# Blocks of the conditioning matrices on ScalarE's transfer queue

## The chip, the cores and the metric

One core of a Trainium2 chip runs the whole kernel in one launch. The metric is device time in microseconds (us), the median of several runs. Five engines matter: TensorE (PE) multiplies, VectorE (DVE) and ScalarE (ACT) do elementwise work, GpSimd (POOL) does sums over partitions and a few powers, and SyncE (SP) only issues transfers. ACT can issue transfers too. Each engine takes its instructions in the order in which they stand in its own stream.

## The reference

An input x of 512 tokens with 1024 features goes through two blocks, each modulated by a conditioning vector c.

```
first block, mod = silu(c) @ ada_w + ada_b        (1024 x 9*1024, cut into 9 pieces sh, sc, g)
  y = rmsnorm(h, g_pre) * (1 + sc1) + sh1
  h = h + 0.5 * g1 * rmsnorm(swiglu(y, w_gate, w_up, w_down), g_post)
  y = rmsnorm(h) * (1 + sc2) + sh2;   h = h + g2 * rmsnorm(mlstm_and_hgrn(y @ w_in) @ w_out)
  a second swiglu with sh3, sc3, g3
second block, twice: mod = silu(c) @ ada_w[l] + ada_b[l]     (1024 x 6*1024, 6 pieces)
  h = h + g * mixer(rmsnorm(h) * (1 + sc) + sh)    (l = 0: gated linear attention,
                                                     l = 1: differential attention)
  h = h + g * (relu(y @ mlp_w1) ** 2) @ mlp_w2     (hidden width 4096)
a final rmsnorm
```

All matrices are float32.

## The kernel before, in words

Every large product is made of three products of a coarse and a fine half of both operands: `fm` (L372 to L374) with the weights as the stationary operand, `tm` (L390 to L392) with the activations as that. A weight matrix comes in `raw` tiles of 1 MB (L333 in `group`, L348 in `group_k`; two buffers). ACT copies the coarse half into a `w` tile (L118 is the line of every ACT instruction), DVE subtracts it from the raw tile for the fine half (L328). There are six `w` tiles. The activations of a layer are kept transposed, in pairs of coarse and fine tiles (`XA...`, `XB...`); L471 and L472 make such a pair from ACT's result `RS`, L611 and L612 (or L606 and L612) make the hidden ones from `tmp`.

The conditioning vectors are made on the side, since each is one row times a matrix of 1024 x 1024. `ada_steps` makes eight steps of each, two halves of 512 columns by four blocks of 256 rows. A step transfers its block of 512 KB into an `araw` tile (L237, two buffers, which the bias rows of L257 and L259 share) and has DVE multiply and add its two halves of 128 rows into `acc` (L241 for the first of a half, L245 for the others). After the fourth block of a half POOL sums `acc` over the partitions (L253), and DVE picks out or adds the bias (L260 to L268). 152 blocks are transferred so. The steps are queued in `jobs`; `work`, called with every product with an estimate of its length, takes one off each 8 us (feed-forward) or 16 us (mixers), so the blocks are spread over the program. The first two pieces of the first block's modulation are needed at once and are made from other strips (L676, eight of them, added by L681 and L683 and summed on PE at L686), which stand with the input and the first weights at the head of SP's stream.

A scheduler sets the order of every engine's stream from the program and from its own estimate of durations; a changed queue therefore moves other instructions too. PSUM has eight banks. In the feed-forward layers six of them hold results of products until ACT or DVE has read them; in the differential attention fewer do: `DIFF_IN_BANKS` names four and `DIFF_BANKS` two. There `d_proj` makes values, queries and keys for four heads at a time; `rope` has ACT copy a product to `tmp` and DVE turn it (L1448 to L1451), PE transposes it (L1546) and ACT copies it into `Y` or `XB`. `diff_X` transposes finished heads (L1525, L1528).

Of the kernel before, what the change touches and what calls it, by code (L numbers as in the profile page):

```python
# [35 lines left out]
def kernel(ctx: ExitStack, tc: tile.TileContext, a: dict, out: bass.AP):  # L36
    nc = tc.nc
# [30 lines left out]
    def sl(tag, dt=F32, w=512):  # L68
        if tag in fixed:
            t = fixed[tag][dt == F32R]  # L70
            return (t if dt in (F32, F32R) else t.bitcast(dt))[:, 0:w]
        return tp.tile([128, w], dt, tag=tag, name=tag, bufs=1)

    def tl(dt=F32, w=512):
        return tp.tile([128, w], dt, tag="tmp", name="tmp", bufs=NTMP)

    def sm(w, tag="sm", bufs=NSM):
        return tp.tile([128, w], F32, tag=tag, name=tag, bufs=bufs)

    def ct(shape, name, dt=F32):  # L80
        return const.tile(shape, dt, tag=name, name=name)
# [23 lines left out]
    def after(ins, first):  # L105
        tc.add_manual_dep(ins.ins, first.ins.name,
                          mybir.DependencyInfo(mybir.DependencyClass.NoSync, mybir.DependencyReason.DATA),
                          reason="activation table")
# [117 lines left out]
    def ada_steps(w, c0, sc, bias, name, post=None, f=1.0):  # L226


        st = {}

        def step(half, kk):
            if kk == 0:
                st["acc"] = tp.tile([128, 512], F32, tag="acc", name="acc", bufs=1)
            acc = st["acc"]
            c = c0 + half * 512
            raw = rawp.tile([128, 2, 512], F32, tag="araw", name="araw", bufs=2)
            nc.sync.dma_start(raw, w[kk * 256:(kk + 1) * 256, c:c + 512].rearrange("(k p) f -> p k f", p=128))  # L237
            for k in range(2):
                col = sc[:, kk * 2 + k:kk * 2 + k + 1]
                if kk == 0 and k == 0:  # L240
                    i = V.tensor_scalar(acc, raw[:, 0, :], col, None, op0=ALU.mult)  # L241
                    if gate:
                        after(i, gate.pop())
                else:
                    V.scalar_tensor_tensor(acc, raw[:, k, :], col, acc, op0=ALU.mult, op1=ALU.add)  # L245
            if kk < 3:
                return
            row = len(bias.shape) == 1
            if half == 0:
                st["r"] = sl("rb", w=D) if row else ct([128, KD], name)  # L250
            r = st["r"]
            red = tl()
            G.partition_all_reduce(red, acc, channels=128, reduce_op=bass_isa.ReduceOp.add)  # L253
            if row:
                hs = slice(half * 512, half * 512 + 512)
                rt = rawp.tile([128, 2, 512], F32, tag="araw", name="araw", bufs=2)
                nc.sync.dma_start(rt[:, 0, :], bias[hs].partition_broadcast(128))  # L257
                if post is not None:
                    nc.sync.dma_start(rt[:, 1, :], post[hs].partition_broadcast(128))  # L259
                V.tensor_tensor(r[:, hs], red, rt[:, 0, :], op=ALU.add)  # L260
                if post is not None:
                    V.scalar_tensor_tensor(r[:, hs], r[:, hs], f, rt[:, 1, :], op0=ALU.mult, op1=ALU.mult)
            else:
                rv = red.rearrange("p (m q) -> p m q", q=128)
                V.tensor_tensor(rv, rv, ident.unsqueeze(1).to_broadcast([128, 4, 128]), op=ALU.mult)
                c4_ = sm(8)[:, 0:4]
                V.tensor_reduce(c4_, rv, axis=AX.X, op=ALU.add)
                V.tensor_tensor(r[:, half * 4:half * 4 + 4], c4_, bias[:, half * 4:half * 4 + 4], op=ALU.add)  # L268
            if half == 1:
                mods[name] = r  # L270
        return [lambda a=a, b=b: step(a, b) for a in range(2) for b in range(4)]

    def bg(n=1):
# [1394 lines left out]
```

## Time and profile before

| | |
|---|---|
| median of 3 runs | 2285.28 us (2283.25 to 2286.25) |
| the profiled execution | 2286.35 us, its span 2284.6 us |
| PE busy | 2225.5 us (97%) |
| DVE busy | 1416.6 us (62%) |
| ACT busy | 923.5 us (40%) |
| POOL busy | 190.2 us (8%) |
| moved by the transfers | 294.69 MB, mean 129 GB/s |
| transfers of the page's list at L237 | 152 of 512 KB, on SP |

The profile is that of one execution. Its times start with the span. A row of the timeline gives the start, the duration, the engine, the line, the operation and the tiles it writes and reads; in square brackets stands how long the engine had been idle before and what it waited for. SPq and ACTq are the issues of transfers: their duration is the issue, not the transfer. When a transfer has landed is seen where an engine that waited for it starts.

### The profile page before, as it was taken

To read this page: it belongs to the slowest core of one execution; us is meant where nothing else is said; L and a number is where in the kernel's file an instruction comes from. 1 tells how busy PE (TensorE), PEld (TensorE's weight loads), DVE (VectorE), ACT (ScalarE), POOL (GpSimd) and SP (SyncE) were. 2 spreads that over 40 slices of the span, in tenths; PEclk is the share of its full clock that TensorE was granted. 3 is DMA by queue.
4 is the path that set the end of the run, shared out by engine and by line. 5 is a ranking of instruction groups with operands and counts; after the bars stand their busy time and mean duration, and the time that the engine had idled before them with its cause. 6 is when DMAs were issued, how large, how long until landed. Compare 5 with 4: busy or idle time off the path is not lost.

```text
span 2284.6 us, 27962 instructions
## 1 busy us (share of the span) xinstructions
PE 2225.5 (97%) x10904; PEld 1839.5 (81%) x10904; DVE 1416.6 (62%) x2371; ACT 923.5 (40%) x1722; POOL 190.2 (8%) x126
## 2 busy tenths in 40 slices
PE   6999999999899999999999999999999999999998
PEld 4888888888788888888888887888776767988887
DVE  7856465765777746555554775568756577634465
ACT  4332234644665332234544443222445456433223
POOL 0111111000101111010000011011000000100000
PEclk9999999999999999999999999999999999999999
DMA  9755454446223655452332254445431311523231
GB/s 272 242 181 181 149 166 74 111 106 105 95 75 111 206 167 179 130 166 76 127 122 92 88 175 156 148 153 157 132 125 55 115 65 50 163 93 102 92 96 61
DMA packets 212900, 294.69 MB, mean 129 GB/s; under 512 B 7257, under 2 KB 120328, under 8 KB 212768
## 3 DMA queue, kind: packets, MB, share of 16 engines
q1 hardware_dynamic: 212128, 291.85, 42.1%
q8 instruction: 85, 1.39, 0.3%
q10 hardware_dynamic: 640, 1.07, 0.1%
q14 instruction: 47, 0.39, 0.1%
HBM read 290.78 MB, written 2.11 MB: 128 GB/s over the span
## 4 chain that ended last, share of the span: by engine, by line
PE 85%; DVE 6%; ACT 3%; DMA 2%; issue 2%; POOL 1%; POOLq 0%; SPq 0%; ACTq 0%; DVEq 0%
PE PS L392 13%; PE PS L390 13%; PE PS L391 13%; PE PS L372 13%; PE PS L373 13%; PE PS L374 13%; PE PS L1474 1%; DVE w L328 1%; ACT RS L118 1%; DMA araw<-in_ada_w_dram 1%; POOL sm L413 1%; PE PS L907 1%; PE PS L1503 1%; ACT tmp L118 1%; ACT w L118 1%
## 5 line engine op out<-in xcount | busy, mean ns | idle before, releaser
L328 DVE TENSOR_TENSOR w<-raw,w 128x1024 fp32r<-128x1024 f32 (+1 forms) x392 | 473.0, 1212 | 396.7 <-ACT w L118 392.4
L118 ACT ACTIVATE w<-raw 128x1024 fp32r<-128x1024 f32 (+1 forms) x392 | 389.3, 1000 | 497.2 <-PE PS L392 278.4
L373 PE MATMUL PS<-XAr,w 128*128 128x512 f32 (+1 forms) x1328 | 482.2, 363 | 1.0 <-DVE XAr L472 0.6
L374 PE MATMUL PS<-XAr,w 128*128 128x512 f32 (+1 forms) x1328 | 481.2, 363 | 0.0
L372 PE MATMUL PS<-XAr,w 128*128 128x512 f32 (+1 forms) x1328 | 480.2, 365 | 0.1
L390 PE MATMUL PS<-w,XAr 128*128 128x512 f32 x806 | 314.3, 391 | 3.2 <-DVE XAr L471 2.2
L391 PE MATMUL PS<-w,XAr 128*128 128x512 f32 x806 | 312.2, 387 | 0.0
L392 PE MATMUL PS<-w,XAr 128*128 128x512 f32 x806 | 310.6, 386 | 0.0
L373 PEld LDWEIGHTS PS<-XAr,w 128*128 128x128 f32 x1328 | 250.2, 188 | 40.9 <-DVE XAr L696 1.3
L372 PEld LDWEIGHTS PS<-XAr,w 128*128 128x128 f32 x1328 | 249.8, 189 | 40.6 <-ACT XAr L118 1.1
L374 PEld LDWEIGHTS PS<-XAr,w 128*128 128x128 f32 x1328 | 249.9, 188 | 38.5
L392 PE MATMUL PS<-w,XBr 128*128 128x512 f32 x704 | 274.3, 390 | 4.1 <-DVE XBr L612 3.6
L391 PE MATMUL PS<-w,XBr 128*128 128x512 f32 x704 | 274.2, 389 | 0.0
L390 PE MATMUL PS<-w,XBr 128*128 128x512 f32 x704 | 274.0, 390 | 0.1
L118 ACT ACTIVATE tmp<-PS 128x512 f32<-128x512 f32 (+3 forms) x227 | 104.3, 465 | 409.0 <-PE PS L374 319.2
L245 DVE SCALAR_TENSOR_TENSOR acc<-araw,silu_c,acc 128x512 f32<-128x512 f32 x266 | 199.3, 749 | 72.2 <-DMA araw<-in_ada_w_dram 67.8
L253 POOL PARTITION_ALL_REDUCE tmp<-acc x38 | 133.4, 3511 | 1040.2 <-DVE acc L245 673.4
L390 PEld LDWEIGHTS PS<-w,XAr 128*128 128x128 f32 x806 | 151.7, 188 | 33.2 <-DVE XAr L471 2.4
L392 PEld LDWEIGHTS PS<-w,XAr 128*128 128x128 f32 x806 | 151.5, 188 | 30.4 <-issue 0.8
L391 PEld LDWEIGHTS PS<-w,XAr 128*128 128x128 f32 x806 | 151.7, 188 | 29.6 <-issue 1.6
L392 PEld LDWEIGHTS PS<-w,XBr 128*128 128x128 f32 x704 | 131.9, 187 | 32.6 <-DVE XBr L612 4.4
L390 PEld LDWEIGHTS PS<-w,XBr 128*128 128x128 f32 x704 | 131.8, 187 | 29.3 <-issue 0.5
(293 smaller groups left out, 2489.0 us busy)
## 6 DMA issues: line engine op xcount, KB each, us to landing
araw<-in_ada_w_dram SPq DMA_DIRECT2D x152, 512.0 KB
raw<-in_mlp_w_dram SPq DMA_DIRECT2D x56, 1024.0 KB
raw<-in_ffn_w_gate_dram SPq DMA_DIRECT2D x20, 1024.0 KB
raw<-in_ffn_w_up_dram SPq DMA_DIRECT2D x20, 1024.0 KB
raw<-in_ffn_w_down_dram SPq DMA_DIRECT2D x20, 1024.0 KB
raw<-in_w_in_dram SPq DMA_DIRECT2D x16, 1024.0 KB
raw<-in_gla_w_in_dram SPq DMA_DIRECT2D x12, 1024.0 KB
raw<-in_diff_w_in_dram SPq DMA_DIRECT2D x12, 1024.0 KB
```

The lines of the kernel that those rows point to most:

```text
L118: ins = S.activation(out, in_, func, **kw)
L245: V.scalar_tensor_tensor(acc, raw[:, k, :], col, acc, op0=ALU.mult, op1=ALU.add)
L253: G.partition_all_reduce(red, acc, channels=128, reduce_op=bass_isa.ReduceOp.add)
L328: V.tensor_tensor(wt[:, 1, ks], src[:, ks], wt[:, 0, ks].bitcast(F32), op=ALU.subtract)
L372: PE.matmul(runs(p), lhsT=wh, rhs=xh, start=k == 0, stop=False)
L373: PE.matmul(runs(p), lhsT=wh, rhs=xl, start=False, stop=False)
L374: done = PE.matmul(runs(p), lhsT=wl, rhs=xh, start=False, stop=k == kn - 1)
L390: PE.matmul(runs(p), lhsT=xh[:, s:s + 128], rhs=wh, start=n == 0, stop=False)
L391: PE.matmul(runs(p), lhsT=xh[:, s:s + 128], rhs=wl, start=False, stop=False)
L392: done = PE.matmul(runs(p), lhsT=xl[:, s:s + 128], rhs=wh, start=False, stop=n == last)
L413: G.tensor_tensor(r, ms, mhalf[:, 0:w], op=ALU.pow)
L907: PE.matmul(p[:, c * 128:(c + 1) * 128], lhsT=L[:, c * 128:(c + 1) * 128], rhs=R[:, c * 128:(c + 1) * 128], start=True, stop=True)
```

## The change

The issue of a block moves from SP's stream to ACT's:

```diff
             raw = rawp.tile([128, 2, 512], F32, tag="araw", name="araw", bufs=2)
-            nc.sync.dma_start(raw, w[kk * 256:(kk + 1) * 256, c:c + 512].rearrange("(k p) f -> p k f", p=128))
+            nc.scalar.dma_start(raw, w[kk * 256:(kk + 1) * 256, c:c + 512].rearrange("(k p) f -> p k f", p=128))
```

All 152 go over. The weights, the bias rows (L257, L259) and everything else stay on SP. In the built program SP has 272 instructions instead of 424 and ACT 1648 instead of 1496. On ACT an issue that waits for a buffer holds up what stands behind it. The scheduler also places other instructions in another order, in a few stretches. Three places follow; a name's number tells tiles of one name apart.

ACT's stream at the program's start, from its table load on. Before:

```order
L114 ACT_TABLE_LOAD
L118 ACTIVATE RS_112,sm_142<-h_129 128x512 x4
L118 ACTIVATE RS_112,sm_157<-h_129 128x512
L118 ACTIVATE Y_111<-h_129,sm_151 128x512
L118 ACTIVATE silu_c_130<-cols0_127 128x8
```

and now:

```order
L114 ACT_TABLE_LOAD
L237 DMA araw_427<-in_ada_w_dram 128x2x512
L118 ACTIVATE RS_112,sm_142<-h_129 128x512
L237 DMA araw_484<-in_ada_w_dram 128x2x512
L118 ACTIVATE RS_112,sm_142<-h_129 128x512 x2
```

The first two blocks (`araw_427`, `araw_484`) now stand behind the table load and behind the first square of the input.

ACT's stream at the queries and keys of the second four heads (`d_proj(1)`). `tmp_13091` and `tmp_13127` are copies of two products, `Y_111` the copies of finished transposes and of head results. Before:

```order
L118 ACTIVATE Y_111<-PS_70,dst_12786 128x128 x4
L118 ACTIVATE tmp_13091<-PS_70 128x512
L118 ACTIVATE tmp_13127<-PS_70 128x512
L118 ACTIVATE Y_111<-PS_70 128x4x128
L118 ACTIVATE tmp_13167<-PS_70 128x512
L118 ACTIVATE Y_111<-PS_70 128x4x128
```

and now:

```order
L118 ACTIVATE Y_111<-PS_70,dst_12786 128x128 x4
L237 DMA araw_13439<-in_ada_w_2_dram 128x2x512
L118 ACTIVATE tmp_13091<-PS_70 128x512
L237 DMA araw_14274<-in_ada_w_2_dram 128x2x512
L118 ACTIVATE Y_111<-PS_70 128x4x128
L118 ACTIVATE tmp_13127<-PS_70 128x512
L118 ACTIVATE XBr5152_512_92<-PS_70,sgc_12033 128x512
```

The issue of `araw_14274`, which waits until DVE is done with `araw_13439`, has come ahead of the copies to `Y_111` and `tmp_13127`.

DVE's stream where the second block's first feed-forward starts. `XAr0` to `XAr6144` are the four groups of its input, `XBr...` hidden tiles, `acc_9553` the sum of a conditioning half. Before:

```order
L471 CAST XAr0_2048_103<-RS_112 128x2x256
L472 TENSOR_TENSOR XAr0_2048_103<-RS_112,XAr0_2048_103 128x2x256
L471 CAST XAr2048_2048_104<-RS_112 128x2x256
L472 TENSOR_TENSOR XAr2048_2048_104<-RS_112,XAr2048_2048_104 128x2x256
L471 CAST XAr4096_2048_105<-RS_112 128x2x256
L245 SCALAR_TENSOR_TENSOR acc_9553<-araw_9879,silu_c2_399,acc_9553 128x512
L472 TENSOR_TENSOR XAr4096_2048_105<-RS_112,XAr4096_2048_105 128x2x256
L471 CAST XAr6144_2048_106<-RS_112 128x2x256
L611 TENSOR_TENSOR tmp_9655<-tmp_9655 128x256
L472 TENSOR_TENSOR XAr6144_2048_106<-RS_112,XAr6144_2048_106 128x2x256
L612 TENSOR_TENSOR XBr4640_512_90<-tmp_9655,XBr4128_512_88 128x256
L245 SCALAR_TENSOR_TENSOR acc_9553<-araw_9879,silu_c2_399,acc_9553 128x512
```

and now:

```order
L611 TENSOR_TENSOR tmp_9614<-tmp_9614 128x256
L245 SCALAR_TENSOR_TENSOR acc_9553<-araw_9879,silu_c2_399,acc_9553 128x512
L471 CAST XAr0_2048_103<-RS_112 128x2x256
L612 TENSOR_TENSOR XBr3608_520_86<-tmp_9614,XBr3088_520_84 128x256
L472 TENSOR_TENSOR XAr0_2048_103<-RS_112,XAr0_2048_103 128x2x256
L471 CAST XAr2048_2048_104<-RS_112 128x2x256
L245 SCALAR_TENSOR_TENSOR acc_9553<-araw_9879,silu_c2_399,acc_9553 128x512
L472 TENSOR_TENSOR XAr2048_2048_104<-RS_112,XAr2048_2048_104 128x2x256
L471 CAST XAr4096_2048_105<-RS_112 128x2x256
L471 CAST XAr6144_2048_106<-RS_112 128x2x256
L472 TENSOR_TENSOR XAr4096_2048_105<-RS_112,XAr4096_2048_105 128x2x256
L472 TENSOR_TENSOR XAr6144_2048_106<-RS_112,XAr6144_2048_106 128x2x256
```

The two L245 on `araw_9879` have moved ahead, the first of them in front of all conversions of the input.

## Rows read from the trace of the kernel before

**Rows 1.** Page: busy us, share, instructions of the engines; the chain's shares.
```profile
PE 2225.5 (97%) x10904; PEld 1839.5 (81%) x10904; DVE 1416.6 (62%) x2371; ACT 923.5 (40%) x1722; POOL 190.2 (8%) x126
...
PE 85%; DVE 6%; ACT 3%; DMA 2%; issue 2%; POOL 1%; POOLq 0%; SPq 0%; ACTq 0%; DVEq 0%
```

**Rows 2.** Windows: stretch, length; PE, PEld, DVE, ACT, POOL busy; clock, DMA share, GB/s.
```profile
10.00:20.00 10.00, 2.67 (x8) 1.57 (x8) 7.22 (x16) 7.78 (x14) 0.86 (x1) 1.00 1.14 325
20.00:30.00 10.00, 6.76 (x23) 5.04 (x24) 9.48 (x23) 2.98 (x5) 0.00 (x0) 0.97 1.20 290
```

**Rows 3.** Waits of SP's queue: line, what it waited for, total us, times, longest.
```profile
SPq L333 <- DVE w L328: 704.0, 80, 31.1
...
SPq L237 <- DVE acc L245: 232.1, 115, 11.3
```

**Rows 4.** Waits of the engines, same columns: DVE for the blocks.
```profile
DVE acc L245 <- DMA araw<-in_ada_w_dram: 67.8, 42, 4.7
```

**Rows 5.** Line L237: count; duration in ns least, median, most; first and last start.
```profile
L237 SPq DMA_DIRECT2D araw<-in_ada_w_dram x152: 367/368/631, 50.3 to 1973.0; - x152
```

**Rows 6.** Timeline, first feed-forward: start, duration, engine, line, tiles, idle before and releaser.
```profile
90.67 1.06 ACT L118 ACTIVATE w<-raw 128x1024 fp32r<-128x1024 f32 x1 [1.44 <-PE PS L374]
...
97.57 6.00 SPq L237 DMA_DIRECT2D araw<-in_ada_w_dram  x2
...
117.57 0.39 PE L372 MATMUL PS<-XAr,w 128*128 128x512 f32 x1
```

**Rows 7.** Timeline of the start.
```profile
12.18 0.35 DVE L681 TENSOR_SCALAR acc<-XBf,silu_c 128x256 f32<-128x256 f32 x1 [0.65 <-DMA XBf<-in_ada_w_dram]
...
14.01 0.88 DVE L445 TENSOR_SCALAR Y<-h,sm 128x512 f32<-128x512 f32 x2 [0.59 <-POOL sm L413]
...
17.95 1.02 PE L686 MATMUL PS<-ones,acc 128*128 128x1 f32 x4 [2.52 <-DVE acc L683]
...
22.05 0.78 PE L372 MATMUL PS<-XAr,w 128*128 128x512 f32 x1
```

**Rows 8.** Timeline, second group of heads, queries and keys.
```profile
1797.29 0.37 SPq L237 DMA_DIRECT2D araw<-in_ada_w_dram  x1
...
1802.57 0.60 ACT L118 ACTIVATE tmp<-PS 128x512 f32<-128x512 f32 x1 [3.17 <-PE PS L392]
...
1803.22 0.48 PE L390 MATMUL PS<-w,XAr 128*128 128x512 f32 x1
...
1803.92 0.75 DVE L245 SCALAR_TENSOR_TENSOR acc<-araw,silu_c,acc 128x512 f32<-128x512 f32 x1 [3.47 <-DMA araw<-in_ada_w_dram]
...
1805.63 0.37 SPq L237 DMA_DIRECT2D araw<-in_ada_w_dram  x1
```

**Rows 9.** Timeline, second block's first feed-forward, end of a conditioning row.
```profile
1405.08 0.37 SPq L237 DMA_DIRECT2D araw<-in_ada_w_dram  x1
...
1409.31 0.75 DVE L245 SCALAR_TENSOR_TENSOR acc<-araw,silu_c,acc 128x512 f32<-128x512 f32 x1 [1.07 <-DMA araw<-in_ada_w_dram]
...
1415.83 0.75 DVE L245 SCALAR_TENSOR_TENSOR acc<-araw,silu_c,acc 128x512 f32<-128x512 f32 x1 [2.76 <-DMA araw<-in_ada_w_dram]
...
1419.08 3.60 POOL L253 PARTITION_ALL_REDUCE tmp<-acc  x1 [45.82 <-DVE acc L245]
...
1419.64 0.49 PE L392 MATMUL PS<-w,XBr 128*128 128x512 f32 x1 [2.06 <-DVE XBr L612]
```

**Rows 10.** Timeline, start of the second block's first feed-forward.
```profile
1309.69 0.37 SPq L237 DMA_DIRECT2D araw<-in_ada_w_dram  x1
...
1318.33 0.75 DVE L245 SCALAR_TENSOR_TENSOR acc<-araw,silu_c,acc 128x512 f32<-128x512 f32 x1 [2.63 <-DMA araw<-in_ada_w_dram]
...
1320.27 0.69 DVE L472 TENSOR_TENSOR XAr<-RS,XAr 128x512 fp32r<-128x512 f32 x1
...
1321.01 0.39 PE L373 MATMUL PS<-XAr,w 128*128 128x256 f32 x1
```

## The prediction

> **What bounds the kernel now.** I read the page first: TensorE (PE) is busy 2225.5 us of 2284.6, ScalarE (ACT) 923.5, and 85% of the chain that ended last is PE [rows 1]. So PE leaves 59.1 us in all; a gain must come out of these, and a cost counts only where PE is made to wait. Next the stretches of the start: PE gets 2.67 of 10 us between 10 and 20 us and 6.76 between 20 and 30, while the DMA engines show shares of 1.14 and 1.20 at 325 and 290 GB/s [rows 2]. The start is bound by transfers, the rest by PE. Then the waits. The queue of SyncE (SP) waits for VectorE (DVE) to release buffers: 704.0 us before the weight loads of L333, 232.1 us in 115 times before those of the conditioning matrices at L237 [rows 3]. What DVE itself waits for these blocks is 67.8 us in 42 times [rows 4]; only a part of it reaches PE.
>
> **What the move removes.** 152 issues of 0.37 us [rows 5] leave SP, 56 us, on an engine that computes nothing: worth nothing by itself. The hoped-for part is that a weight load no longer stands behind a block that waits. I followed the weight loads of L333 and L348 in SP's order: except for one at 82 us, which has time in hand, each goes out when the wait for its own raw buffer ends, and that is the wait of the 704.0 us. The blocks, too, go out when their own buffer (two of them) is released by L245. I cost this at 0.
>
> **What it adds on ACT.** 56 us of issue on an engine busy for 923.5 us, and 152 in-order waits, mostly for DVE's L245. Whatever ACT has behind a waiting issue waits too. In the feed-forward bodies that is covered: the issue of 97.57 us now stands ahead of the conversion that ran at 90.67, so it is held 6.9 us and 0.4 for the issue, but PE multiplies with that weight first at 117.57 [rows 6]; with DVE's step on it in between, some 15 us of cover are left. The results of the products have six PSUM banks there. Without that cover such a hold would cost its whole 7 us. Five places lack cover.
>
> **A, the start.** ACT now issues the first two blocks right behind its table load and its first square (fence on ACT's start), at about 4 and 5 us, in place of 50.3 us [rows 5]. Each is 0.52 MB. DMA is full there, so 1.05 MB go in ahead of the first strips that SP has in flight: 1.05 MB / 325 GB/s = 3.2 us, or / 290 = 3.6 us [rows 2]. Those strips feed the chain that PE waits for: DVE starts on them at 12.18 after a wait for the DMA, PE's L686 waits 2.52 us for the sum and runs at 17.95, the first product is at 22.05 [rows 7]. Of the delay DVE can take back 0.59 us, its wait for GpSimd (POOL) at 14.01 [rows 7], since the second half's norm will be ready by then. So +2.6 to +3.0; I take **+2.8**, bounds +2.2 (the second block still partly beside work that waits anyway) to +3.6. From 40 us on PE runs without a pause, so the loss stays.
>
> **B, the queries and keys of the second head group (1797 to 1807 us).** The issue that SP made at 1805.63, when both L245 on the block before had ended, now stands on ACT ahead of the copy that ran at 1802.57 and one into Y (fence on ACT at 1803 us); PE's next product, at 1803.22, waits for the PSUM bank that the copy of 1802.57 frees [rows 8]. The block before was issued at 1797.29 and was there at 1803.92: 6.6 us [rows 8]. Now its issue stands behind ACT's four copies into Y and goes out at about 1798.9. With the shortest latency that I show, 4.2 us (issued 1405.08, used 1409.31 after a wait for it) [rows 9], it lands at 1803.1; with 6.6 us at 1805.5. Then two L245 at 0.7 us from start to start, 0.4 for the issue, and the two copies at 0.5 from start to start and 0.6 at the end [rows 8]: the bank is free at 1806.0 to 1808.4 instead of 1803.2, so 2.8 to 5.2 us. PE's order has six transposes of 0.12 us moved into this gap, 0.7 less. Bounds +2.1 to +4.5; **+3.1**, nearer the short latency, since the weight load ahead of it is 2 us older.
>
> **C, the first feed-forward of the second block (1310 to 1321 us).** L245 on a block issued at 1309.69 ran at 1318.33, when it landed, 8.6 us later; from there to the end of the last conversion L472 (1320.27 plus 0.69) were 2.6 us, and PE's L373 followed at 1321.01 [rows 10]. In the new order of DVE (fence on DVE at 1312 us) that L245, a second one, all eight steps of the conversions and an L612 stand one behind the other: two L245 at 0.7, four L471 at 0.4, four L472 at 0.6 and L612 at 0.4, with 0.1 for the last end, make 5.9 us from the landing (L472 takes 0.69 [rows 10] and the steps overlap a little). With the same landing that is 3.3 us late; with a landing 5.3 us after the issue nothing is. The 6.6 us of B give **+1.3**, bounds 0 to +3.3.
>
> **D, the end of a conditioning row (1405 to 1420 us).** Here PE waits 2.06 us for DVE's L612, which sits behind an L245 that waited 2.76 us for its block; from the landing at 1415.83 to PE's 1419.64 are 3.8 us [rows 9]. A block that came sooner would give that back. But in the new order L265, which waits for POOL's all-reduce of 3.60 us [rows 9], stands ahead of L612: two L245 (1.4), the all-reduce (3.6), L265 and L612 (0.7 each, about as L472 [rows 10]) make 6.4 us from the landing. With the landing unchanged +2.6; it breaks even 2.6 us sooner, and the shortest latency, from an issue at about 1409.0 behind ACT's copies, gives -0.3 or so. I take **+0.8**.
>
> **E, the rest.** At 720, 906, 412, 518, 1626, 1670 and 1940 us an issue or a reordered L245 falls into stretches where a wait of at most 1 or 2 us comes or goes. I could not give these a sign: **0**, bounds -2.5 to +2.5, an estimate from the size of D's wait, 2.06 us [rows 9].
>
> The landings in B, C and D rest on one question: does a block on its own queue pass a 1 MB load that was issued ahead of it? No row shows two queues loading at once, as nearly all loads were SP's. The Trainium skill, DMA: Bandwidth & Descriptors, section "Queues, rings and completion order", says that each engine takes turns between queues packet by packet, so a block would pass. By it alone the sums would be B +2.1, C 0, D -0.3, A as it is: 4.6 in place of 8.0.
>
> **Sum.** 2.8 + 3.1 + 1.3 + 0.8 + 0 = 8.0 us on the profiled execution of 2286.35 us (span 2284.6 and 1.75 around it), which is 1.07 above the median of 2285.28. So 2294.35 there, **2293.3 us** as a median. The sum of the low bounds is 2.2 + 2.1 + 0 - 0.3 - 2.5 = 1.5, of the high ones 3.6 + 4.5 + 3.3 + 2.6 + 2.5 = 16.5: 2286.8 to 2301.8.
>
> **Rivals.**
> *Nothing to measure.* The blocks' bytes and DVE's work are the same, the first blocks do not disturb the strips (their packets wait), and the copies of B happen to be done before ACT reaches the waiting issue. Then 56 us of issue vanish under ACT's idle time: 2285 to 2288. For it: 15 us of cover at the one hold shown [rows 6]. Against it: DMA shares over 1 at the start [rows 2], and ACT's strict order in B. The Trainium skill, same page, section "Issuing engines are not separate DMA queues", points here too: all issuers share 16 DMA engines, and only issue time is saved; the shares over 1 at the start agree that there is no second supply of bandwidth.
> *Faster.* The second queue lets every block land in 4.2 us instead of up to 8.6 [rows 9, 10], at places like 1417 us; the 67.8 us of DVE [rows 4] shrink, and with them PE's stalls of 2 us behind them. Three such stalls make -6 us, and if A and B are hidden too: 2279. It decides at a landing 2.6 us sooner at D and needs A to be absent, against [rows 2].
> *A cascade.* The 232.1 us that SP waited for L245 [rows 3] now stand on ACT, 2.0 us each. If two more places like B (a PSUM copy behind a waiting issue, no spare bank) exist in the mixers, +4 each on the sum: 2301 and above. It decides where the hold exceeds the spare banks.
>
> **Chances.** Forecast 0.60, nothing to measure 0.21, faster 0.08, cascade 0.11. A measurement of this kernel tells about 0.2% from no change, 2280.7 to 2289.9. Of the forecast's case some 0.12 lies below 2289.9. So faster 0.07, same 0.33, slower 0.60. For eight in ten: from 2284 (nothing to measure, mostly) to 2300, leaving out the fast case and most of the cascade.
>
> **What would show it.** A: the first product later than 22.05 by 2 to 4 us, strips landing later. B: PE idle some 3 us near 1803 with a copy on ACT as its releaser, and on ACT a wait before an issue. C and D: L472 and L265 as last releasers near 1321 and 1420, shifted by the gain or loss before them. No change in SP's waits before L333. Wrong would be: PE's first product at 22 us, or holds on ACT that no PE wait follows.

## The result and the profile after

The changed kernel takes 2302.0 us (median of 6 runs, 2299.99 to 2304.53) against 2285.72 for the kernel before in the same session: ratio 1.0073, interval 1.0060 to 1.0086. It is slower by 16.3 us. The prediction had the sign, but 8.0 us for the size, and a range that ended at 2300. The profiled execution took 2300.69 us, its span 2299.0 (2286.35 and 2284.6 before).

Page of the changed kernel: busy time of the engines, and the shares of the chain that ended last.

```profile
PE 2230.0 (97%) x10904; PEld 1841.9 (80%) x10904; DVE 1421.1 (62%) x2371; ACT 921.5 (40%) x1722; POOL 191.3 (8%) x126
...
PE 83%; DVE 8%; DMA 3%; ACT 3%; issue 2%; POOL 1%; ACTq 0%; POOLq 0%; DVEq 0%
```

Beside [rows 1] nothing on the page tells of 16 us. Two readings hide in it. PE is idle 69.0 us instead of 59.1, and it is *busy* 4.5 us longer with the same 10904 instructions: some of its products ran slower.

To find the places I matched PE's products of the two traces one by one by their place in the program and took how much later each begins. That lag grows in steps: +2.5 us by 25 us (A), +2.1 near 1320 (C), +4.4 at 1421 to 1432 (D), +7.1 at 1803 to 1822 (B); everything else adds up to -1.8. Together that is 14.3 us between the two profiled executions.

Waits of the changed kernel (what was waited for, total us, times, longest), those of its engines that bear on the change:

```profile
DVE acc L245 <- DMA araw<-in_ada_w_dram: 78.8, 53, 4.9
ACT w L118 <- DVE acc L245: 64.8, 10, 18.1
...
ACT Y L118 <- DVE acc L245: 19.0, 4, 7.9
...
PE PS L392 <- DVE XBr L612: 5.8, 2, 5.1
PE PS L390 <- ACT tmp L118: 4.8, 1, 4.8
```

ACT now waits for L245, as expected, and by far the most before conversions into `w`. DVE waits for the blocks 78.8 us in 53 times instead of 67.8 in 42 [rows 4]: the blocks did not come sooner. PE's own waits show two new long ones, 5.1 and 4.8 us. They are D and B.

**A.** Windows of the start (stretch, length; PE, PEld, DVE, ACT, POOL busy; clock, DMA share, GB/s), and the timeline rows that answer to [rows 7]:

```profile
10.00:20.00 10.00, 1.56 (x4) 0.55 (x3) 4.51 (x13) 4.73 (x10) 0.93 (x1) 1.00 1.12 334
20.00:30.00 10.00, 6.82 (x20) 5.19 (x20) 9.82 (x19) 4.35 (x6) 0.00 (x0) 1.00 1.19 292
```

```profile
14.91 0.35 DVE L681 TENSOR_SCALAR acc<-XBf,silu_c 128x256 f32<-128x256 f32 x1 [4.75 <-DMA XBf<-in_ada_w_dram]
...
17.93 0.88 DVE L445 TENSOR_SCALAR Y<-h,sm 128x512 f32<-128x512 f32 x2 [0.59 <-POOL sm L413]
...
20.31 1.01 PE L686 MATMUL PS<-ones,acc 128*128 128x1 f32 x4 [0.96 <-DVE acc L683]
...
24.54 0.78 PE L372 MATMUL PS<-XAr,w 128*128 128x512 f32 x1
```

The DMA engines are as full as in [rows 2], and DVE's first step on the strips moves from 12.18 to 14.91 us: 2.7 us of other bytes went in ahead. In the packets of the trace these are ACT's two blocks, issued at 2.2 and 4.6 us: their 1.05 MB land between 6 and 12 us, and from 8 to 11 us SP's own queue falls to between 79 and 218 GB/s, against 290 to 357 in before; both queues together move 376 to 390 GB/s there instead of 290 to 343. PE's first product moves from 22.05 to 24.54.

**B.** Timeline of the second head group, queries and keys (against [rows 8]), and windows of the same columns as above:

```profile
1806.45 0.37 ACTq L237 DMA_DIRECT2D araw<-in_ada_w_dram  x1
...
1813.34 1.54 DVE L245 SCALAR_TENSOR_TENSOR acc<-araw,silu_c,acc 128x512 f32<-128x512 f32 x2 [4.42 <-DMA araw<-in_ada_w_dram]
...
1814.91 0.38 ACTq L237 DMA_DIRECT2D araw<-in_ada_w_dram  x1
1815.34 0.60 ACT L118 ACTIVATE Y<-PS 128x512 f32<-128x512 f32 x1 [7.86 <-DVE acc L245]
1815.83 0.59 ACT L118 ACTIVATE tmp<-PS 128x512 f32<-128x512 f32 x1
...
1816.47 0.79 PE L390 MATMUL PS<-w,XAr 128*128 128x512 f32 x1 [4.82 <-ACT tmp L118]
1817.06 0.63 PE L391 MATMUL PS<-w,XAr 128*128 128x512 f32 x1
1817.49 0.63 PE L392 MATMUL PS<-w,XAr 128*128 128x512 f32 x1
```

```profile
1817.00:1819.00 2.00, 2.00 (x6) 1.55 (x5) 1.66 (x4) 0.58 (x1) 0.00 (x0) 0.50 0.44 167
1819.00:1821.00 2.00, 2.00 (x6) 1.52 (x6) 0.00 (x0) 0.00 (x0) 0.00 (x0) 0.50 0.00 0
...
1823.00:1825.00 2.00, 2.00 (x12) 1.50 (x10) 0.00 (x0) 0.52 (x2) 0.00 (x0) 1.00 0.00 0
```

The chain reads from top to bottom: issue at 1806.45, landing 6.9 us later, two L245, the waiting issue of 1814.91, then ACT's copies, idle for 7.86 us before the first of them, then PE after a pause of 4.82. What I had not foreseen stands in the windows: the granted clock is 0.50 behind the pause, the lower level of 1.2 GHz, and 6 products fit where 12 do at 1.00. Eleven products start 0.43 us apart instead of 0.23: 2.2 us more.

**D.** Timeline of the end of the conditioning row (against [rows 9]), and a window:

```profile
1422.25 1.54 DVE L245 SCALAR_TENSOR_TENSOR acc<-araw,silu_c,acc 128x512 f32<-128x512 f32 x2 [2.78 <-DMA araw<-in_ada_w_dram]
...
1423.88 4.14 POOL L253 PARTITION_ALL_REDUCE tmp<-acc  x1 [46.80 <-DVE acc L245]
1424.85 2.73 DVE L611 TENSOR_TENSOR tmp<-tmp 128x512 f32<-128x512 f32 x1
1428.06 0.69 DVE L265 TENSOR_TENSOR tmp<-tmp,ident 128x512 f32<-128x512 f32 x1 [0.48 <-POOL tmp L253]
1428.66 0.68 DVE L612 TENSOR_TENSOR XBr<-tmp,XBr 128x512 fp32r<-128x512 f32 x1
...
1429.40 0.80 PE L392 MATMUL PS<-w,XBr 128*128 128x512 f32 x1 [5.08 <-DVE XBr L612]
```

```profile
1429.00:1431.00 2.00, 1.60 (x4) 1.32 (x5) 2.00 (x6) 0.00 (x0) 0.00 (x0) 0.50 0.65 226
```

L265 waits for POOL ahead of L612, so PE waits 5.08 us instead of 2.06, and again the clock behind the pause is 0.50. The two things add 3.0 and some 1.4 us.

**C.** Timeline rows that answer to [rows 10]:

```profile
1313.99 0.37 ACTq L237 DMA_DIRECT2D araw<-in_ada_w_dram  x1
...
1322.02 0.75 DVE L245 SCALAR_TENSOR_TENSOR acc<-araw,silu_c,acc 128x512 f32<-128x512 f32 x1 [4.94 <-DMA araw<-in_ada_w_dram]
...
1324.10 0.38 PE L373 MATMUL PS<-XAr,w 128*128 128x256 f32 x1 [0.55 <-DVE XAr L472]
```

The block lands 7.9 us after its issue, and with the first of its steps now ahead of all conversions DVE stands 4.94 us, where it stood 2.63 [rows 10].

### The profile page after: what moved, and what is told of

Read it like the earlier page. It is cut to its first block, busy times and chain, and to the rows that moved or that the text cites. A ratio compares the mean times of both kernels' runs of the same rounds, so it can differ in the third digit from the quotient of the medians.

```text
span 2299.0 us, 27927 instructions
## 1 busy us (share of the span) xinstructions
PE 2230.0 (97%) x10904; PEld 1841.9 (80%) x10904; DVE 1421.1 (62%) x2371; ACT 921.5 (40%) x1722; POOL 191.3 (8%) x126
## 3 DMA queue, kind: packets, MB, share of 16 engines
q8 instruction: 85, 1.39, 0.3%
HBM read 290.78 MB, written 2.11 MB: 127 GB/s over the span
## 4 chain that ended last, share of the span: by engine, by line
PE 83%; DVE 8%; DMA 3%; ACT 3%; issue 2%; POOL 1%; ACTq 0%; POOLq 0%; DVEq 0%
PE PS L373 13%; PE PS L372 13%; PE PS L374 13%; PE PS L392 12%; PE PS L390 12%; PE PS L391 12%; DMA araw<-in_ada_w_dram 2%; DVE w L328 2%; PE PS L1474 1%; POOL sm L413 1%; DVE acc L245 1%; PE PS L907 1%; ACT RS L118 1%; PE PS L1503 1%; ACT tmp L118 1%
## 5 line engine op out<-in xcount | busy, mean ns | idle before, releaser
L328 DVE TENSOR_TENSOR w<-raw,w 128x1024 fp32r<-128x1024 f32 (+1 forms) x392 | 479.4, 1228 | 390.7 <-ACT w L118 386.2
L390 PE MATMUL PS<-w,XAr 128*128 128x512 f32 x806 | 314.6, 391 | 7.1 <-ACT tmp L118 4.8
L392 PE MATMUL PS<-w,XAr 128*128 128x512 f32 x806 | 311.4, 387 | 0.0
L392 PE MATMUL PS<-w,XBr 128*128 128x512 f32 x704 | 275.4, 392 | 6.4 <-DVE XBr L612 5.8
L390 PE MATMUL PS<-w,XBr 128*128 128x512 f32 x704 | 274.9, 391 | 0.1
L245 DVE SCALAR_TENSOR_TENSOR acc<-araw,silu_c,acc 128x512 f32<-128x512 f32 x266 | 199.2, 749 | 82.5 <-DMA araw<-in_ada_w_dram 78.8
L390 PEld LDWEIGHTS PS<-w,XAr 128*128 128x128 f32 x806 | 151.9, 188 | 37.5 <-ACT tmp L118 5.4
L392 PEld LDWEIGHTS PS<-w,XAr 128*128 128x128 f32 x806 | 151.7, 188 | 30.4 <-issue 0.8
L392 PEld LDWEIGHTS PS<-w,XBr 128*128 128x128 f32 x704 | 132.3, 188 | 35.5 <-DVE XBr L612 6.7
```

The costliest lines, as they stand in the source:

```text
L328: V.tensor_tensor(wt[:, 1, ks], src[:, ks], wt[:, 0, ks].bitcast(F32), op=ALU.subtract)
L390: PE.matmul(runs(p), lhsT=xh[:, s:s + 128], rhs=wh, start=n == 0, stop=False)
L392: done = PE.matmul(runs(p), lhsT=xl[:, s:s + 128], rhs=wh, start=False, stop=n == last)
```

## The experiments

Blocks are numbered in the order in which they are issued, 0 to 151: 0 and 1 are those of A, 99 that of C, 111 that of D, 144 the issue that waits in B. Most experiments send chosen blocks through SP again:

```diff
-            nc.scalar.dma_start(raw, w[kk * 256:(kk + 1) * 256, c:c + 512].rearrange(...))
+            n = turn_no[0]
+            turn_no[0] += 1
+            queue = nc.scalar if n not in (0, 1) else nc.sync
+            queue.dma_start(raw, w[kk * 256:(kk + 1) * 256, c:c + 512].rearrange(...))
```

The table has the medians; "before" is the kernel before in the same session.

| kernel | on ACT | us | before | ratio, interval |
|---|---|---|---|---|
| the changed kernel | all 152 | 2302.00 | 2285.72 | 1.0073 [1.0060, 1.0086] |
| e1 | all but 0, 1 | 2301.25 | 2287.17 | 1.0066 [1.0051, 1.0081] |
| e2 | all but 144 | 2295.18 | 2287.17 | 1.0042 [1.0028, 1.0056] |
| e3 | all but 111 | 2295.03 | 2287.17 | 1.0042 [1.0029, 1.0056] |
| e4 | all but 99 | 2298.96 | 2287.17 | 1.0055 [1.0040, 1.0070] |
| e5 | all but 0, 1, 99, 111, 144 | 2285.87 | 2284.55 | 1.0002 [0.9993, 1.0011] |
| e6 | 0, 1, 99, 111, 136 to 144 | 2300.70 | 2284.55 | 1.0069 [1.0057, 1.0082] |
| e7 | all, L265 behind L612 in D | 2301.24 | 2284.55 | 1.0072 [1.0056, 1.0089] |
| e8 | all, pause of B filled | 2302.92 | 2284.55 | 1.0081 [1.0068, 1.0095] |
| e9 | all, L245 behind L612 in D | 2296.09 | 2284.98 | 1.0038 [1.0026, 1.0051] |
| e10 | 136 to 144 | 2291.50 | 2284.98 | 1.0022 [1.0013, 1.0030] |
| e11 | 136 to 144, pause of B filled | 2289.19 | 2284.98 | 1.0017 [1.0009, 1.0026] |
| e12 | all but 0, 1, 99, 144; D as e9 | 2281.39 | 2285.39 | 0.9982 [0.9973, 0.9991] |

**One place at a time (e1 to e4).**

```diff
+            queue = nc.scalar if n not in (0, 1) else nc.sync     (e1; e2: n != 144, e3: n != 111, e4: n != 99)
```

> All blocks go out on ACT but the first two, which are back on SP; the scheduler puts DVE's and ACT's start back as it was before the change. Theory of places (the loss of 16 us sits at the start, in B, C and D, and nowhere else): the first product is back near 22 us and the lag of 2.5 us that PE has by 40 us in the trace of the changed kernel is gone, so 2.5 us less than 2302.0: about 2299.5, later places as in the changed kernel. Theory of spread cost (152 issues of 0.37 us on ACT and the shared bandwidth cost 0.1 us each): two of 152 blocks give back 0.2 us, 2301.8.

> One block of 152, the one whose issue stands ahead of the two copies in B (the first of the last conditioning row), is back on SP. Theory of places: ACT no longer waits for DVE there, the pause of PE of 4.8 us near 1811 us and the half clock behind it are gone, 7.1 us less than 2302.0: about 2294.9. Theory of spread cost: 0.1 us less, 2301.9.

> One block of 152 is back on SP, the one that DVE waits for in D; the scheduler then puts DVE's L265 behind L612 again and one L245 behind L611. Theory of places with the order as the cause: the pause of 5.1 us near 1424 us shrinks to about 2 us as before the change and the half clock behind it goes, 4.4 us less than 2302.0: about 2297.6, although the block itself lands as late as it does now, some 7.2 us after its issue. Theory that the second queue is the cause (sharing delays the landing): the landing comes earlier by the 2 us or more that the pause grew. Theory of spread cost: 0.1 us less, 2301.9.

> One block of 152 is back on SP, the one that DVE waits for in C; the scheduler then puts the first L245 on it behind the first four steps of the conversions again. Theory of places: PE's lag does not grow by 2.1 us near 1320 us, 2.1 us less than 2302.0: about 2299.9. Theory of spread cost: 0.1 us less, 2301.9.

Against the 16.3 us of the full change the distances to before are 14.1, 8.0, 7.9 and 11.8 us. With intervals of about 3 us to either side the two of e2 and e3 stand clear of the full change; e1 and e4 alone do not, and rest on their traces; e1's median is even nearer to the theory of spread cost (2301.8) than to that of places (2299.5), and e3's is 2.6 us below its forecast. What the four give back (2.2, 8.3, 8.4 and 4.5 us) adds up to 23.4, more than the whole loss; "before" stood some 1.5 us higher in their session, and a single time here is good to some 2 us. In the traces the step of the place is gone or smaller each time: -2.0 us at the start in e1, -7.7 at B in e2, -2.6 at D in e3, -2.5 at C in e4. The rest of such a trace also wanders by 2 us, near 575 us, where PE pauses 5.0 to 6.8 us in every kernel, and near 1680 us, where it pauses 1.7 to 3.0 us in all kernels but the changed one (1.4).

e3 separates two explanations of D. Its block, on SP again, still lands 7.6 us after the issue (1413.78 to 1421.35), yet PE's pause falls from 5.08 to 2.15 us, since L612 is back ahead of what waits for POOL. The later landing is not the cause; the order is. PE in e3 (shifted lines: L394 to L396 are L390 to L392, L616 is L612):

```profile
1425.25 0.50 PE L396 MATMUL PS<-w,XBr 128*128 128x512 f32 x1 [2.15 <-DVE XBr L616]
...
1425.82 0.56 PE L395 MATMUL PS<-w,XBr 128*128 128x512 f32 x1
1426.17 0.63 PE L396 MATMUL PS<-w,XBr 128*128 128x512 f32 x1
```

The clock fell behind this pause too, while behind the 2.06 us of before [rows 9] it stayed at 1.00 (products 0.22 apart). That is why e3's trace gives back 2.6 us at D and not 4.4; it is the slowest of e3's five executions (2300.68 us). C has no such test of its own: its block landed sooner than in before (7.9 us after the issue instead of 8.6), so a later landing is not its cause either, but the order alone was not run there.

**The five together, and only they (e5, e6).**

```diff
+            queue = nc.scalar if n not in (0, 1, 99, 111, 144) else nc.sync          (e5)
+            queue = nc.scalar if n in (0, 1, 99, 111) or 136 <= n < 145 else nc.sync (e6)
```

> The blocks of e1 to e4 together, five of 152, are back on SP; 147 stay on ACT. Theory of places: the four losses go (2.5 + 2.1 + 4.4 + 7.1 = 16.1 us in the trace of the changed kernel) and what else the change moved comes to about 0, so the time is that of the kernel before, 2284 to 2288 us, though ACT issues 147 blocks and waits for DVE before most of them. Theory of spread cost (56 us of issue on ACT, its 150 waits, the shared bandwidth): 147 of 152 parts of the loss stay, about 2301.

> The other way round: all blocks on SP as in the kernel before, but thirteen go out on ACT: the first two, those of C and D, and the nine of the last quarter-row before and at B; the scheduler's order at the start and in B, C and D is then that of the changed kernel. Theory of places: nearly the whole loss comes with these 13, 16 us over the kernel before: about 2302. Theory of spread cost: 13 of 152 parts, 1.4 us over it: about 2288.

This is the pair that settles where the time went. 147 blocks on ACT cost nothing (1.0002), and 13 cost what all 152 do (1.0069 against 1.0073). e6's lag has the same steps: +2.9 at the start, +2 near C, +4.7 at D, +6.6 at B. (Nine blocks up to 144 are on ACT in e6, and with them the scheduler puts the waiting issue ahead of the two copies; whether fewer would do was not run.) What e5 leaves on ACT still waits there:

```profile
ACT w L118 <- DVE acc L249: 58.6, 7, 17.3
...
ACT tmp L118 <- DVE acc L249: 19.8, 6, 6.3
ACT Y L118 <- DVE acc L249: 17.9, 4, 6.5
```

These are e5's waits (its lines stand four further down). 96 us of in-order waits on ACT, up to 17.3 us at a time, and no time lost: that is cover, measured.

**The order in D (e7, e9).** e7 puts the instruction that waits for POOL behind L612; e9 puts the two L245 on block 111 behind it, so that POOL itself starts later.

```diff
 in ffn's hidden:
+            hid.append(V.tensor_tensor(hx[1][:, s:s + n], ...))       (L612)
 in ada_steps, e7:
+                picked = V.tensor_tensor(rv, rv, ident..., op=ALU.mult)   (L265)
+                if n == 111:
+                    after(picked, hid[-1])
 in ada_steps, e9:
+                    i = V.scalar_tensor_tensor(acc, raw[:, k, :], col, acc, ...)   (L245)
+                    if n == 111 and k == 0:
+                        after(i, hid[-1])
```

> All blocks on ACT as in the changed kernel; only the order on DVE in D is pinned, L265 stands behind L612 again; the two L245 stay next to each other. If the order is the cause in D, the pause of 5.1 us near 1424 us shrinks to some 3 us (the second L245 still stands ahead, 0.7), with the landing unchanged at about 7 us after the issue: 2 us less for the pause, and up to 1.4 more where the clock does not fall: 2298.5 to 2300. If the second queue is the cause (a late landing), the pause stays near 5 us: 2302.

> The changed kernel with one order more: the two multiplies of DVE (L245) on the last block of the conditioning row at 1405 to 1420 us (block 111) have to stand behind the hidden layer's last subtraction (L612), where they stood before the change; the block stays on ScalarE's queue. Theory 'the order costs it': DVE no longer waits for the landing ahead of the subtraction, GpSimd's all-reduce doesn't start before it, TensorE's pause there falls from 5.08 us to about the 2.1 us of before, and of the 4.4 us that the place costs 2.4 to 4.4 come back: 2297.6 to 2299.6 us. Rival 'the later landing costs it' (the block lands 7.2 us after its issue whichever way): the pause stays near 5 us and the time at 2302.

e7 missed: 16.7 us above before, as the full change. DVE and POOL in its trace (shifted lines: L618, L619 are L611, L612):

```profile
1421.23 2.73 DVE L618 TENSOR_TENSOR tmp<-tmp 128x512 f32<-128x512 f32 x1
1424.44 0.49 DVE L246 TENSOR_SCALAR acc<-araw,silu_c 128x512 f32<-128x512 f32 x1 [0.48 <-POOL tmp L258]
1424.85 0.69 DVE L619 TENSOR_TENSOR XBr<-tmp,XBr 128x512 fp32r<-128x512 f32 x1
```

```profile
1420.28 4.13 POOL L258 PARTITION_ALL_REDUCE tmp<-acc  x1 [47.60 <-DVE acc L250]
```

Another instruction took L265's place: the first multiply of the next half (L246 here, L241 in the original), which must wait until POOL has read the single `acc`. And the L618 ahead of it takes 2.73 us instead of 0.68, because it runs beside POOL. So it was not one instruction's place but POOL's early start.

e9 takes that away and gives 5 us back (11.1 above before instead of 16.3; the intervals do not touch); 2296.09 is 1.5 us below the forecast. In its trace PE has no pause at D at all, not even the 2.06 us of before. The expectation had one thing wrong: in before, too, both L245 stood ahead of L612, the first with its wait of 2.76 us [rows 9], the second as here:

```profile
1418.23 0.75 DVE L245 SCALAR_TENSOR_TENSOR acc<-araw,silu_c,acc 128x512 f32<-128x512 f32 x1
1418.90 0.69 DVE L612 TENSOR_TENSOR XBr<-tmp,XBr 128x512 fp32r<-128x512 f32 x1
```

e9's trace also has a shorter pause at B, 2.82 us, with the block there landing 5.4 us after its issue; so not all of the 5 us need be D's.

**B alone, and the clock (e8, e10, e11).** e10 is the kernel before with nine blocks on ACT. e8 and e11 have PE work through the pause of B on 22 products that nobody reads; e8 does it in the full change, e11 in e10.

```diff
+            queue = nc.scalar if n in range(136, 145) else nc.sync            (e10, e11)
 in d_proj, behind the rope that leaves the pause (e8, e11):
+                if hg == 1 and u == 0 and blk == 1:
+                    for _ in range(22):
+                        i = PE.matmul(PS[:, 3584:4096], lhsT=X5[0][0][:, 0:128], rhs=X5[0][0], start=True, stop=True)
+                    filled.append(i)
```

> The changed kernel with 22 products more, whose results nobody reads, put on PE into the pause of B; ACT's wait is as long as before, and the six transposes that had come forward stand later again (0.7 us). If the half clock behind a pause of 4.8 us is a cost of its own, the 11 products that then started each 0.43 us instead of 0.23 run at full clock: 2.2 less and 0.7 more, about 1.5 us less than 2302.0, so 2300.5, and the granted clock stays at 1.00 near 1817 us. If those products are slow for another reason, nothing changes or the work adds to the time: 2302 to 2303.

> The kernel before with nine blocks alone on ScalarE's queue (136 to 144, up to the one whose transfer DVE waits for in the second head group, at 1800 to 1822 us), all others on SyncE's. Theory 'the ordered wait of that one issue costs TensorE a pause of 4.8 us and 2.2 us of slow products behind it': before plus 6.5 to 7.5 us, 2292 to 2293.5. Rival 'the losses need one another (the load of the whole queue)': under 4 us, below 2289.7.

> The same nine blocks, and 22 products whose result nobody reads, put in TensorE's pause in the second head group. Theory 'TensorE's clock, halved after the pause, is 2.2 us of the loss': the products right behind the pause start 0.23 us apart instead of 0.43, the granted clock there reads 1.00, and the time is 1.5 to 2.5 us below that of the nine blocks without the filling: 2290 to 2291.5. Rival 'the products are slow for another reason (their operands, the transfers at that moment)': 0.43 us apart, same time as without, or 0.5 us more.

e10 stands 6.5 us above before by the medians, 5.0 by the ratio, with an interval of 3 to 7: B costs without the other places, though not surely its whole 7.1 us. Its profiled execution was the shortest of its 12 (2285.67 us), and shows B at its mildest: PE in e10 (its lines stand four further down), and two windows.

```profile
1802.14 0.48 PE L394 MATMUL PS<-w,XAr 128*128 128x512 f32 x1 [2.72 <-ACT tmp L118]
```

```profile
1803.00:1805.00 2.00, 2.00 (x8) 1.53 (x7) 1.33 (x3) 0.24 (x1) 0.00 (x0) 0.61 0.28 104
1805.00:1807.00 2.00, 2.00 (x7) 1.58 (x6) 0.00 (x0) 0.00 (x0) 0.00 (x0) 0.54 0.00 0
```

The pause is 2.72 us, and the block of B landed 5.4 us after its issue instead of 6.9. Six products run at full speed, then the clock falls all the same and eight start 0.43 apart. With the filling, e11:

```profile
1799.99 5.28 PE L1563 MATMUL PS<-XAr 128*128 128x512 f32 x22
1806.43 0.48 PE L395 MATMUL PS<-w,XAr 128*128 128x512 f32 x1 [1.16 <-ACT tmp L118]
1806.76 0.38 PE L398 MATMUL PS<-w,XAr 128*128 128x512 f32 x1
```

```profile
1807.00:1809.00 2.00, 2.00 (x11) 1.71 (x10) 0.39 (x2) 0.00 (x0) 0.00 (x0) 1.00 0.38 144
```

The clock stays at 1.00, and the products behind the pause start 0.22 apart: the lower clock comes from PE standing still, and not from the operands or the transfers. Only this spacing can be compared between the two traces, since the block of B landed 7.4 us after its issue in e11's. e11's median is 2.3 us below e10's, as the theory had it, but the two intervals overlap widely, so the times alone do not prove it. e8 missed its forecast of 2300.5: the filling took 2.2 us off at B in the trace (the clock reads 1.00 from 1811 to 1825), while its time, 2302.92, was no lower than that of the full change. Two other places of that execution were 2.7 and 1.3 us slower than in the changed kernel's; the first is the pause near 1680 us that the changed kernel's trace has shorter than all others. Whether the rest is scatter is not shown. That the lower clock costs some 2 us at B is shown by the traces; in the times it is only likely.

**A version that beats both (e12).** Blocks 0, 1, 99 and 144 go back to SP, 111 stays on ACT with the order of e9.

> Blocks 0, 1, 99 and 144 on SyncE's queue, the other 148 on ScalarE's, and the order of the run before last at block 111 (both multiplies behind the hidden layer's last subtraction). The run with five blocks on SyncE stood at the time of before; with the order, TensorE's pause at 1417 to 1420 us is gone altogether, where before has 2.06 us. Theory 'what is left of the change costs nothing and the pause was on the path': 1.5 to 3 us below before, 2282 to 2283.8. Rival 'a later wait takes the 2 us back': the time of before, within 1 us.

2281.39 us, 4.0 below before and 0.6 below the forecast, 0.9982 [0.9973, 0.9991]: faster than both. DVE at D in e12, and a window of it:

```profile
1412.43 0.68 DVE L618 TENSOR_TENSOR tmp<-tmp 128x512 f32<-128x512 f32 x1
1413.15 0.69 DVE L619 TENSOR_TENSOR XBr<-tmp,XBr 128x512 fp32r<-128x512 f32 x1
1413.76 1.53 DVE L250 SCALAR_TENSOR_TENSOR acc<-araw,silu_c,acc 128x512 f32<-128x512 f32 x2
```

```profile
1414.00:1416.00 2.00, 2.00 (x11) 1.71 (x10) 1.85 (x3) 0.00 (x0) 0.62 (x1) 1.00 0.94 269
```

L619 (L612 of the original) stands ahead of the multiplies, and PE runs through, with 2.3 us gained at D against before. e5, the same but for block 111 and its order, stood at the time of before. So the gain comes with block 111: with its order on DVE by the trace, since on ACT without that order it costs (D). The order alone, on the kernel before with all blocks on SP, was not run, so what part the queue has in it is not shown; what makes it 4 us rather than 2.3 stays open too, within a scatter of 1 to 2 us.

## Why the prediction was right and wrong

**What bounds the kernel: right.** 56 us of issues left SP and gained nothing; e5 shows 147 blocks moved at no cost and no gain. One sign I gave was wrong: SP's waits before L333 did change, from 704.0 [rows 3] to 881.5 us:

```profile
SPq L333 <- DVE w L328: 881.5, 81, 31.0
```

SP gets to a weight load sooner and waits for the buffer there itself, which moves no load: against the lag that PE has at that moment, the issues of the 198 loads of L333 and L348 are shifted by 0.0 us in the median. Such a wait says how early a queue arrives, not what it costs.

**Cover in the feed-forward: right.** The holds of up to 18 us before conversions cost nothing.

**A: right, the number partly by luck.** Forecast +2.8, measured +2.5 at the first product, by the mechanism given (1.05 MB ahead of the strips); e1 takes 2.0 of it back in the trace. Two parts erred and nearly cancel: the strips came 2.7 us later and not 3.2 to 3.6, as the two queues together moved more than SP's alone had (whether the second queue does that or its packets of 2 KB is not shown), and DVE did not take back the 0.59 us, since it still waits 0.59 us for POOL (the row of 17.93). Nor does PE run without a pause from 40 us on, it waits 6.7 us near 575 us in both kernels; but its lag does not shrink there (1.5 us ahead of that pause, 2.4 behind it).

**The landings: wrong, and three terms rested on it.** I had let a block on its own queue land after 4.2 to 6.6 us. At B, C and D it took 6.9, 7.9 and 7.2 us. The 4.2 us belonged to a block that was issued 1.8 us *ahead* of a weight load (1405.08 against 1406.85 us), not behind one; the blocks of B, D and C in before (issued at 1797.29, 1408.27 and 1309.69) went out 0.7 to 1.7 us behind a load and took 6.6, 7.5 and 8.6 us. At B, C and D, too, each was issued 1.4 to 2.0 us behind a 1 MB weight load on SP's queue, and in none did it pass: the loads landed at 1813.09, 1320.19 and 1420.88, the blocks at 1813.32, 1321.92 and 1422.16. Over the 150 blocks after 60 us the mean from issue to landing went from 4.87 to 4.80 us. The Trainium skill, DMA: Bandwidth & Descriptors, section "Queues, rings and completion order", says that the engines take turns between queues packet by packet. The trace does not refute that: at B load and block end 0.2 us apart, as sharing would have it. What was wrong was the step from there to "the block passes", and with it the 4.6 us that the prediction drew from it. With another queue the DMA engines had no more to give: at B, from 1804 to 1810 us, they moved 320 to 395 GB/s at shares of 0.91 to 1.03, in the same stretch of before (1797 to 1803) 388 to 400 at 1.03 to 1.05.

**B: right mechanism, wrong size.** Forecast +3.1 with bounds 2.1 to 4.5. The pause is 4.82 us, just past the upper bound, since the landing took a little more than the 6.6 us that made it; e10 and e9 with landings of 5.4 us have pauses of 2.7 and 2.8, which is the value I took. The other 2.2 us, the slow products behind it, had no term at all.

**D: right order, wrong choice in it.** The sum said +2.6 with the landing unchanged, and I took +0.8 in the hope of an earlier one (whose low end is 0.0 by its rows, not -0.3). Unchanged it was (7.2 us, 7.5 before), and the pause grew by 3.0: the 6.4 us from landing to PE became 7.2, of which 0.5 is POOL's all-reduce at 4.14 instead of 3.60 us. The lower clock behind the pause made it 4.4. e3 shows the order as the cause, e7 that L265 was only one of two instructions that wait for POOL there, e9 what takes both away.

**C: right**, +2.1 between 0 and 3.3, above the +1.3 again because of the landing (7.9 us, not 6.6).

**E: right**, -1.8 within 2.5 of nothing. Most of it lies near 1675 us, one of the places named: PE pauses 1.39 us there instead of 2.21, and the clock behind the pause stays at 1.00 where it fell to 0.50 in before. Most other kernels with blocks on ACT have the longer pause again, so it is more likely scatter than the change.

**The sum.** A, B, C, D and E came to 2.5, 7.1, 2.1, 4.4 and -1.8, that is 14.3 instead of 8.0 (16.3 by the medians). Some 3.6 of the 6.3 missing are the clock behind B and D (2.2 and 1.4), about 4.5 the landings and what hangs on them (B's pause 1.8, D's 2.2, C's 0.8, less 0.3 that A was cheaper), and E takes 1.8 off. The upper end of the range, 2300, left out the sum of the high bounds (16.5 us, 2301.8), which is where the time fell.

**The rivals.** "Nothing to measure" fell at A, "faster" at the landings. The cascade gave the right time for another reason: no further place like B appeared, and three of the four known places cost more than forecast.

## What to carry to other kernels

A transfer issued from a computing engine is a wait in that engine's stream. 147 of 152 cost nothing here, and the places of five cost 16 us; look for the places where the next copy frees the only bank, and for the first microseconds. Only B is such a wait on ACT: A is bytes that go in ahead, and D, probably C too, an order on DVE that the scheduler changed along with the queue, so read the new order of every engine. A pause of a TensorE that is otherwise always busy should be priced with the products behind it: here 4.8 us of waiting cost 7.0. And before hoping that a second queue brings data sooner, look at what the DMA engines already move at that moment, and take a latency from a row that stood behind the same kind of load.

## What the runs showed of the hardware beyond what was expected

- **TensorE's clock after a pause.** Behind pauses of 4.82 and 5.08 us it was granted 0.50 (1.2 GHz) for some 4.9 and 2.9 us; behind 2.72 us (e10) the windows read 0.61 and 0.54 after six products at full speed, behind 2.15 us (e3) and 2.11 us (e11, at D) it fell to the lower level too, and behind 2.06 us (before, at D) it stayed at 1.00. It fell behind a still shorter pause as well, one of 1.83 us in e10 (0.50 from 1671 to 1673 us):

```profile
1669.96 0.50 PE L394 MATMUL PS<-w,XAr 128*128 128x512 f32 x1 [1.83 <-DVE XAr L475]
```

So the length of the pause alone does not decide; what does is open. With PE kept busy through the pause (e8, e11) it stayed at 1.00.
- **DVE beside GpSimd's all-reduce.** A multiply of a tile with itself (L611, 128x512) takes 0.68 us, and 2.73 where it starts 0.8 to 1.1 us after POOL's sum over the partitions has, in all 66 such cases of the 14 traces. The sum took 4.0 to 4.3 us there (4.14 at D, 4.13 in e7), 3.60 in before and 3.23 in e9, with less of DVE beside it. The Trainium skill, SBUF — State Buffer, section "Who interferes with whom", says that a DVE instruction with two inputs in SBUF contends with a GpSimd instruction that reads SBUF. The rows agree, 2.73 us against 0.68. The multiply looks held up rather than slowed throughout: in all 66 cases it ended 0.44 or 0.45 us before the sum, and an L612 that started 1.1 us after a sum of only 3.24 us took 1.70 us and ended 0.45 us before it too. POOL's spans are rough in this profile, and what releases DVE at that point is not shown.
